# RWKV block inverse by doubling: products and copies on 64 strided columns in place of 128

## The chip, the cores and the metric

One Trainium2 chip, of which the program uses one core. The metric is the device time of one execution in microseconds; the kernel before took 3047.91 us, the median of three runs (3046.5 to 3051.92).

## The reference, cut to what matters

Two transformer blocks in float32 on 512 tokens of width 1024. The first block mixes a forgetting attention (8 heads) with an RWKV-7 recurrence (8 heads of 64) and ends with a gated feed-forward layer; the second has two further linear recurrences and a product-key mixture of 16384 experts. The change is in the RWKV recurrence alone:

```python
def step(S, inp):
    r_t, w_t, k_t, v_t, a_t, b_t = inp
    Sa = jnp.einsum('bhij,bhj->bhi', S, a_t)
    S = S * w_t[:, :, None, :] + Sa[..., None] * b_t[:, :, None, :] + v_t[..., None] * k_t[:, :, None, :]
    return S, jnp.einsum('bhij,bhj->bhi', S, r_t)
```

The kernel does not walk the 512 steps. It cuts the tokens into chunks of 64, and within a chunk the rank-one term makes a triangular system: a unit lower triangular matrix has to be inverted for each chunk and head.

## The kernel before, in words

Weights stream from HBM through a ring of tiles (`_load`, `_split`, `next_w`), and the program runs through its stages one after the other: normalisation and projections with the attention between them, then the RWKV stage, then output projection, feed-forward, the second block and the experts. Work is given in program order, but the order in which each engine gets its instructions is made when the program is built: L1679 opens the block with `schedule_with_timeline_sim=True`, and a planner orders the instructions of each engine by the times that it simulates. The splits of weights are traced at high priority. Each engine then runs its list strictly in that order and waits on semaphores.

The RWKV stage (L1576 to L1598) handles 8 units: 4 pairs of heads by 2 groups of 4 chunks. For each unit, `rwkv_elem` (once for two units) makes decays and keys, `rwkv_group` (L726 to L794) builds the matrices, among them `NT` with four blocks of 128x128, each holding two 64x64 triangles on its diagonal (the two heads), `rwkv_inv` (L796 to L832) inverts them, `rwkv_fold` multiplies the inverse into the transfer matrices (L841, L848), and `rwkv_scan` (L867) steps through the four chunks. The loop prepares unit u+2 and inverts unit u+1 while unit u is folded and scanned.

`rwkv_inv` runs for two halves of a unit side by side (`run_all`, h = 0 and 1), with two 128x128 blocks each. It keeps `T`, the inverse so far, and its transpose `Tt`. It begins with blocks of 2 (L813 to L817), and then doubles for m = 2, 4, 8, 16, 32. A level is: product `NT`ᵀ`T` for both blocks into PSUM (L809), copy to `Y` on ScalarE (L823), product `Tt`ᵀ`Y` into PSUM (L809), a masked copy into `T` on VectorE under the mask `lv` of that level (L826), and, except in the last level, two transposes (L812) and a copy to `Tt` on ScalarE (L830). The mask picks, in each square of 2m, the lower left square of m: rows of the second half, columns of the first half. All other columns of the product are computed and thrown away.

PSUM: the half h has one bank tag, `i0` in A and `i1` in B, two buffers each (L57). `cu` (L337 to L339) and `lv` (L382 to L384) are the masks, loaded from the constant `cu` in `consts` and `attn_consts` on SyncE's DMA queue; the slices of `cu` also serve `hgrn` (L1010) up to n = 32.

In the trace the digits of tile names are left out (`T0` and `T1` are `T`; the PSUM tiles `i0` and `i1` are `i`). A product in float32 stands as two weight loads and two matmul records.

Of the kernel before, what the change touches and what calls it, by code (L numbers as in the profile page):

```python
# [12 lines left out]
U32 = mybir.dt.uint32  # L13
# [46 lines left out]
def shape_consts():  # L60
    p = np.arange(128)
    out = {}
    ident = np.eye(128, dtype=np.float32)
    blk = (p[:, None] // 64 == p[None, :] // 64).astype(np.float32)
    s64 = p % 64
    t64 = np.arange(64)
    rmask = np.concatenate([s64[:, None] < t64[None], s64[:, None] <= t64[None]], 1).astype(np.float32)
    out["cf"] = np.concatenate([ident, blk, rmask, np.where(p[None] <= p[:, None], 0, -1e30).astype(np.float32)], 1)

    def lev(m, strict_same=128):  # L70
        same = p[:, None] // (2 * m) == p[None, :] // (2 * m)
        return same & (p[:, None] % (2 * m) >= m) & (p[None, :] % (2 * m) < m)
    us = [lev(m) for m in (2, 4, 8, 16, 32)] + [lev(m).T for m in (1, 2, 4, 8, 16, 32, 64)]
    out["cu"] = np.concatenate(us, 1).astype(np.uint32)
    scm = np.ones((128, T), np.float32)
    scm[:, ::64] = 0.0
    out["cs"] = scm
    out["ic"] = np.concatenate([ident[:64, :64], ident[64:, 64:]], 0)
    out["io"] = np.broadcast_to(np.arange(128, dtype=np.float32), (128, 128))
    inv = np.float32(10000.0) ** (-np.arange(128, dtype=np.float32) / np.float32(128))  # L80
    ang = np.arange(T, dtype=np.float32)[None, :] * inv[:, None]
    gam = 1.0 - 2.0 ** (-5.0 - np.arange(4))
    rel = np.arange(T)[None, :] - p[:, None]
    mr = np.where(rel[None] >= 0, gam[:, None, None] ** np.maximum(rel, 0)[None], 0.0)
    out["c2"] = np.concatenate([np.cos(ang)[None], np.sin(ang)[None], mr]).astype(np.float32)
    return out


def prep(inp):
# [58 lines left out]
    for h in range(4):  # L148
# [13 lines left out]
    o["bvec"] = np.stack([g["attn_norm_post"][0], g["ffn_norm_post"][0], g["final_norm_w_2"], g["norm_ffn_w_2"][0],  # L162
                          g["attn_norm_pre"][0], g["ffn_norm_pre"][0], g["norm_mix_w_2"][0]])
    o.update(shape_consts())
    return {k: np.ascontiguousarray(v) for k, v in o.items()}

class Prog:
# [45 lines left out]
    def v(self, name, i=0, rows=slice(0, 128)):  # L215
        o, n = VEC[name]
        return self.vec[rows, o + i:o + i + 1]
# [111 lines left out]
    def consts(self):  # L329
        nc, I, cp = self.nc, self.I, self.cp  # L330
        ld = nc.sync.dma_start
        nv = I["vec"].shape[1]
        self.vec = cp.tile([128, nv], F32, name="vec")
        ld(self.vec, I["vec"])
        self.identb = cp.tile([128, 128], BF16, name="identb")
        nc.vector.tensor_copy(self.identb, self.ident)
        self.cu = cp.tile([128, 7, 128], U32, name="cu")  # L337
        ld(self.cu, I["cu"].rearrange("p (m n) -> p m n", n=128)[:, 5:12])
        self.levTt = {1: 0, 2: 1, 4: 2, 8: 3, 16: 4, 32: 5, 64: 6}  # L339
        self.iota = cp.tile([128, 128], F32, name="iota")  # L340
        ld(self.iota, I["io"])

        dv = cp.tile([128, 56], F32, name="dv")
        self.dv = dv
        V = lambda n: self.vec[:, VEC[n][0]:VEC[n][0] + VEC[n][1]]
        ts = nc.vector.tensor_scalar
        ts(dv[:, 0:4], V("mu_r"), -1.0, 1.0, op0=ALU.mult, op1=ALU.add)
        ts(dv[:, 4:8], V("mu_k"), -1.0, 1.0, op0=ALU.mult, op1=ALU.add)
        ts(dv[:, 8:12], V("mu_v"), -1.0, 1.0, op0=ALU.mult, op1=ALU.add)
        ts(dv[:, 12:15], V("mu_l"), -1.0, 1.0, op0=ALU.mult, op1=ALU.add)  # L350
        ts(dv[:, 16:20], V("w0"), 0.5, None, op0=ALU.mult)
        ts(dv[:, 20:24], V("a0"), 0.5, None, op0=ALU.mult)
        ts(dv[:, 24:28], V("k_a"), 0.5, None, op0=ALU.mult)
        ts(dv[:, 28:29], V("fb"), -1.0, None, op0=ALU.mult)
        ts(dv[:, 32:40], V("hgw"), 0.5, None, op0=ALU.mult)

        nc.vector.tensor_tensor(dv[:, 40:48], V("lb0"), V("lb1"), op=ALU.max)
        lw = cp.tile([128, 4, 8], F32, name="lw")
        nc.vector.tensor_tensor(lw[:, 0], V("lb0"), dv[:, 40:48], op=ALU.subtract)
        nc.vector.tensor_tensor(lw[:, 1], V("lb1"), dv[:, 40:48], op=ALU.subtract)  # L360
        nc.scalar.activation(lw[:, 0:2], lw[:, 0:2], AF.Exp)
        nc.vector.tensor_tensor(lw[:, 2], lw[:, 0], lw[:, 1], op=ALU.add)
        nc.vector.reciprocal(lw[:, 2], lw[:, 2])
        nc.vector.tensor_tensor(lw[:, 3], lw[:, 0], lw[:, 2], op=ALU.mult)

        nc.vector.tensor_scalar(dv[:, 40:48], lw[:, 3], -0.5, 0.5, op0=ALU.mult, op1=ALU.add)
        nc.vector.tensor_tensor(dv[:, 48:56], lw[:, 3], dv[:, 40:48], op=ALU.add)
        self.eps = cp.tile([128, 1], F32, name="eps")
        nc.vector.memset(self.eps, NORM_EPS)
        self.ones = cp.tile([128, 128], F32R, name="ones")  # L370
        nc.scalar.activation(self.ones, self.ident, AF.Copy, bias=1.0, scale=0.0)

    def attn_consts(self):

        nc, I = self.nc, self.I
        ld = nc.sync.dma_start
        cf = self.b("ac", [128, 384])
        ld(cf, I["cf"][:, 128:512])
        self.blk, self.rmask = cf[:, 0:128], cf[:, 128:256]
        self.causb = self.b("causb", [128, 128], BF16)  # L380
        nc.vector.tensor_copy(self.causb, cf[:, 256:384])
        self.lv = self.b("lv", [128, 5, 128], U32)  # L382
        ld(self.lv, I["cu"].rearrange("p (m n) -> p m n", n=128)[:, 0:5])
        self.levT = {2: 0, 4: 1, 8: 2, 16: 3, 32: 4}  # L384
        self.ic = self.b("ic", [128, 64])
        ld(self.ic, I["ic"])
        self.cs = self.b("ac")
        ld(self.cs, I["cs"])
        self.rkblk = self.b("ac", [128, 4, 128])
        for c in range(4):  # L390
            nc.vector.tensor_scalar(self.rkblk[:, c, :], self.blk, self.v("r_k", c), None, op0=ALU.mult)
# [404 lines left out]
    def rwkv_inv(self, e, g_, h):  # L796

        nc = self.nc
        B = [128, 2, 128]
        nt = e["G", g_]["nt"][:, 2 * h:2 * h + 2]  # L800
        tt, tf = self.S(B, name=f"Tt{h}"), self.S(B, name=f"T{h}")
        mask = lambda t_, i: t_[:, i, None, :].to_broadcast(B)

        def each(op, out, *a):
            for i in range(2):
                op(out[:, i], *[x[:, i] for x in a])

        def product(out, a, b):
            nc.tensor.matmul(out, a, b, start=True, stop=True)  # L809

        def transpose(out, a):
            nc.tensor.transpose(out, a, self.ident)  # L812
        nc.gpsimd.tensor_copy(tt, self.ident[:, None, :].to_broadcast(B))  # L813
        nc.vector.copy_predicated(tt, mask(self.cu, self.levTt[1]), nt)
        pt = self.b(f"i{h}", B)
        each(transpose, pt, tt)
        nc.scalar.activation(tf, pt, AF.Copy)  # L817
        yield
        for m in (2, 4, 8, 16, 32):
            py = self.b(f"i{h}", B)  # L820
            each(product, py, nt, tf)
            y = self.S(B, name=f"Y{h}")
            nc.scalar.activation(y, py, AF.Copy)  # L823
            px = self.b(f"i{h}", B)
            each(product, px, tt, y)
            nc.vector.copy_predicated(tf, mask(self.lv, self.levT[m]), px)  # L826
            if m < 32:
                pt = self.b(f"i{h}", B)
                each(transpose, pt, tf)
                nc.scalar.activation(tt, pt, AF.Copy)  # L830
            yield
        e["G", g_]["tf", h] = tf  # L832
# [850 lines left out]
```

## Time and profile before

| what | value |
|---|---|
| median of 3 runs | 3047.91 us |
| the profiled execution, its own time | 3051.43 us |
| its span, first to last instruction | 3049.5 us |
| mean granted TensorE clock | 0.988 |
| TensorE busy with matmuls / weight loads | 2937.2 / 2539.3 us |
| VectorE, ScalarE, GpSimd busy | 1868.9, 1230.8, 1456.4 us |

PE is TensorE's matmuls, PEld its weight loads, which overlap them; DVE is VectorE, ACT ScalarE, POOL GpSimd, SP SyncE. Ends of matmuls are modelled, so the starts tell the pace better than the busy time. The page cuts the span into 40 slices of 76 us; the RWKV stage lies in the fourth to sixth, from about 240 to 450 us. PEclk is the granted clock, 1.00 for 2.4 GHz and 0.50 for 1.2 GHz.

### The profile page before, as it was taken

How to read it: one execution, taken by the hardware profiler on the slowest of the kernel's cores; microseconds unless marked ns; L12 is line 12 of the kernel's file. 1: busy time of each engine (PE TensorE's matmuls, PEld its weight loads, DVE VectorE, ACT ScalarE, POOL GpSimd, SP SyncE). 2: the span in 40 equal slices, each digit the busy share in tenths (PEclk: the TensorE clock that was granted, in tenths of full speed). 3: DMA queues.
4: the chain of work that ended last, by engine and by line, in shares of the span. 5: the costliest groups of instructions: out<-in, count | busy, mean ns of one | idle time of the engine just before them, and what ended most of it. 6: DMA issues, size and time to landing. Idle time of an engine off the chain costs nothing.

```text
span 3049.5 us, 40450 instructions
## 1 busy us (share of the span) xinstructions
PE 2937.2 (96%) x15129; PEld 2539.3 (83%) x15129; DVE 1868.9 (61%) x3173; ACT 1230.8 (40%) x1924; POOL 1456.4 (48%) x1070
## 2 busy tenths in 40 slices
PE   7998998999999999999999998998999999999998
PEld 6877787888878887888888878997899999999877
DVE  4237664444133663355532499788688777877898
ACT  5455654222232453244432334566333333333333
POOL 3223213222234562233332345676677777777764
PEclk9999999999999999999999999999999999999999
DMA  4220003333332212322233422455988888898987
GB/s 154 63 63 15 1 32 101 97 97 97 97 111 84 69 42 69 107 87 83 83 106 112 135 70 88 141 187 196 313 302 290 317 305 301 299 317 299 319 316 249
DMA packets 174355, 473.62 MB, mean 155 GB/s; under 512 B 15056, under 2 KB 64592, under 8 KB 172624
## 3 DMA queue, kind: packets, MB, share of 16 engines
q1 hardware_dynamic: 137296, 336.80, 34.0%
q0 software_dynamic: 36864, 134.23, 12.4%
q8 instruction: 120, 1.97, 0.3%
q14 instruction: 75, 0.61, 0.1%
HBM read 439.49 MB, written 31.46 MB: 154 GB/s over the span
## 4 chain that ended last, share of the span: by engine, by line
PE 63%; DVE 8%; issue 5%; DMA 4%; POOL 3%; ACT 1%; POOLq 0%; DVEq 0%; SPq 0%; ACTq 0%
PE acc L270 12%; PE acc L271 12%; PE acc L272 12%; DMA urow<-ev,ei 3%; PE A L272 3%; PE A L271 3%; PE A L270 3%; PE B L271 3%; PE B L270 3%; PE B L272 3%; PE pg L1388 2%; POOL urow L1336 1%; PE lev L986 1%; DVE mux L1315 1%; DVE wk L1233 1%
## 5 line engine op out<-in xcount | busy, mean ns | idle before, releaser
L247 POOL TENSOR_TENSOR lo<-raw,hi 128x1024 fp32r<-128x1024 f32 x224 | 557.1, 2488 | 819.0 <-ACT hi L244 783.2
L270 PE MATMUL acc<-u,hi 128*128 128x512 f32 (+3 forms) x2344 | 859.4, 367 | 12.5 <-ACT x L1403 8.6
L271 PE MATMUL acc<-u,hi 128*128 128x512 f32 (+3 forms) x2344 | 856.6, 366 | 0.2 <-DVE u L476 0.2
L272 PE MATMUL acc<-u,lo 128*128 128x512 f32 (+3 forms) x2344 | 855.5, 365 | 0.0
L244 ACT ACTIVATE hi<-raw 128x1024 fp32r<-128x1024 f32 x447 | 473.2, 1059 | 882.9 <-PE acc L271 446.7
L270 PEld LDWEIGHTS acc<-u,hi 128*128 128x128 f32 (+1 forms) x2344 | 444.5, 190 | 67.4 <-ACT x L1403 9.2
L247 DVE TENSOR_TENSOR lo<-raw,hi 128x1024 fp32r<-128x1024 f32 x223 | 311.6, 1398 | 297.4 <-ACT hi L244 297.1
L271 PEld LDWEIGHTS acc<-u,hi 128*128 128x128 f32 (+1 forms) x2344 | 444.6, 190 | 53.8 <-issue 2.7
L272 PEld LDWEIGHTS acc<-u,lo 128*128 128x128 f32 (+1 forms) x2344 | 444.2, 190 | 49.1 <-issue 0.6
L1344 DVE SCALAR_TENSOR_TENSOR urow<-urow,h4row 128x1024 f32<-128x1024 f32 x128 | 201.0, 1578 | 90.9 <-DMA urow<-eu,ei 90.2
L1354 DVE SCALAR_TENSOR_TENSOR po<-urow,act,po 128x1024 f32<-128x1024 f32 x127 | 200.8, 1581 | 71.7 <-DMA urow<-ev,ei 70.6
L1336 POOL DMA_INDIRECT urow<-eu,ei x128 | 188.5, 1472 | 33.1 <-issue 23.7
L1414 ACT ACTIVATE wh<-wf 128x384 fp32r<-128x384 f32 x128 | 67.4, 528 | 322.0 <-PE D L271 244.6
L1336 POOL DMA_INDIRECT urow<-ev,ei x128 | 174.4, 1362 | 44.8 <-DVE po L1354 18.7
L247 POOL TENSOR_TENSOR lox<-rawx,hix 128x1024 fp32r<-128x1024 f32 x53 | 138.4, 2612 | 96.5 <-ACT hix L244 96.2
L1390 ACT ACTIVATE gstage<-pg 128x512 f32<-128x512 f32 x96 | 99.1, 1107 | 60.3 <-PE pg L1388 59.7
L1379 DVE TENSOR_SCALAR ohA<-iota,slT 128x128 f32<-128x128 f32 x384 | 117.4, 371 | 2.3 <-ACT slT L1364 1.1
L1388 PE MATMUL pg<-ohB,ohA 128*128 128x128 f32 x768 | 100.4, 278 | 15.1 <-DVE ohB L1385 7.7
L1388 PEld LDWEIGHTS pg<-ohB,ohA 128*128 128x128 f32 x768 | 94.8, 191 | 19.7 <-ACT gstage L1390 10.5
L1383 POOL TENSOR_SCALAR ohB<-iota,slT 128x128 f32<-128x128 f32 x144 | 95.9, 681 | 26.4 <-PE pg L1388 26.4
L1415 DVE TENSOR_TENSOR wl<-wf,wh 128x384 fp32r<-128x384 f32 x128 | 98.9, 774 | 5.7 <-ACT wh L1414 3.8
L1385 DVE TENSOR_TENSOR ohB<-iota,slT 128x512 f32<-128x512 f32 x60 | 66.4, 1107 | 33.7 <-PE pg L1388 33.5
(573 smaller groups left out, 5473.5 us busy)
## 6 DMA issues: line engine op xcount, KB each, us to landing
raw<-ut SPq DMA_DIRECT2D x128, 512.0 KB
raw<-ev SPq DMA_DIRECT2D x75, 512.0 KB
rawx<-ev SPq DMA_DIRECT2D x53, 512.0 KB
raw<-w_ret SPq DMA_DIRECT2D x48, 512.0 KB
gd<-gstage SPq DMA_DIRECT2D x12, 2048.0 KB
gread<-gd SPq DMA_DIRECT2D x32, 768.0 KB
raw<-w_gu SPq DMA_DIRECT2D x44, 512.0 KB
raw<-w_hg SPq DMA_DIRECT2D x32, 512.0 KB
```

The costliest lines, as they stand in the source:

```text
L244: self.nc.scalar.activation(hi, raw, AF.Copy)
L247: r = eng.tensor_tensor(lo, raw, hi.bitcast(F32), op=ALU.subtract)
L270: mm(out, a[0], b[0], start=start, stop=False)
L271: mm(out, a[0], b[1], start=False, stop=False)
L272: return mm(out, a[1], b[0], start=False, stop=stop).ins
L1336: r = nc.gpsimd.indirect_dma_start(out=u, out_offset=None, in_=src, in_offset=bass.IndirectOffsetOnAxis(ap=ei[:, s:s + 1], axis=0))
L1344: nc.vector.scalar_tensor_tensor(u, u, 1.0, row, op0=ALU.mult, op1=ALU.mult, accum_out=act[:, s:s + 1])
L1354: nc.vector.scalar_tensor_tensor(o, u, act[:, s:s + 1], o, op0=ALU.mult, op1=ALU.add)
L1379: nc.vector.tensor_scalar(A4[:, r], self.iota, sl[:, 0, k + r:k + r + 1], sl[:, 2, k + r:k + r + 1], op0=ALU.is_equal, op1=ALU.mult)
L1388: last = nc.tensor.matmul(p[:, r, :], A4[:, r], B4[:, r], start=True, stop=True)
L1390: nc.scalar.activation(st[:, :, q * 4:q * 4 + 4].rearrange("p j t -> p t j"), p, AF.Copy)
L1415: nc.vector.tensor_tensor(wl, wf, wh.bitcast(F32), op=ALU.subtract)
```

## The change

In each level only the columns that the mask can pick are computed: the first m columns of every 2m, 64 of 128. `T` is viewed as blocks of 2m columns and `first` is the first half of each. The first product takes `first` as its moving operand, with gaps; its output, `Y`, the second product and its output are dense tiles of 64 columns for each of the two blocks. The masked copy goes from the dense product into `first`, with gaps, under masks of 64 columns, which are a new constant `cl`. The stationary operands (`NT`, `Tt`) stay 128x128, and transposes and the copies to `Tt` stay as they are. The constant `cu` keeps six slices (it had twelve, of which seven and five were loaded).

```diff
--- before.py
+++ after.py
@@ -70,8 +70,11 @@
     def lev(m, strict_same=128):
         same = p[:, None] // (2 * m) == p[None, :] // (2 * m)
         return same & (p[:, None] % (2 * m) >= m) & (p[None, :] % (2 * m) < m)
-    us = [lev(m) for m in (2, 4, 8, 16, 32)] + [lev(m).T for m in (1, 2, 4, 8, 16, 32, 64)]
+    us = [lev(m).T for m in (1, 2, 4, 8, 16, 32)]
     out["cu"] = np.concatenate(us, 1).astype(np.uint32)
+
+    out["cl"] = np.concatenate([lev(m).reshape(128, 64 // m, 2, m)[:, :, 0].reshape(128, 64) for m in (2, 4, 8, 16, 32)],
+                               1).astype(np.uint32)
     scm = np.ones((128, T), np.float32)
     scm[:, ::64] = 0.0
     out["cs"] = scm
@@ -334,9 +337,9 @@
         ld(self.vec, I["vec"])
         self.identb = cp.tile([128, 128], BF16, name="identb")
         nc.vector.tensor_copy(self.identb, self.ident)
-        self.cu = cp.tile([128, 7, 128], U32, name="cu")
-        ld(self.cu, I["cu"].rearrange("p (m n) -> p m n", n=128)[:, 5:12])
-        self.levTt = {1: 0, 2: 1, 4: 2, 8: 3, 16: 4, 32: 5, 64: 6}
+        self.cu = cp.tile([128, 6, 128], U32, name="cu")
+        ld(self.cu, I["cu"].rearrange("p (m n) -> p m n", n=128))
+        self.levTt = {1: 0, 2: 1, 4: 2, 8: 3, 16: 4, 32: 5}
         self.iota = cp.tile([128, 128], F32, name="iota")
         ld(self.iota, I["io"])
 
@@ -379,8 +382,8 @@
         self.blk, self.rmask = cf[:, 0:128], cf[:, 128:256]
         self.causb = self.b("causb", [128, 128], BF16)
         nc.vector.tensor_copy(self.causb, cf[:, 256:384])
-        self.lv = self.b("lv", [128, 5, 128], U32)
-        ld(self.lv, I["cu"].rearrange("p (m n) -> p m n", n=128)[:, 0:5])
+        self.lv = self.b("lv", [128, 5, 64], U32)
+        ld(self.lv, I["cl"].rearrange("p (m n) -> p m n", n=64))
         self.levT = {2: 0, 4: 1, 8: 2, 16: 3, 32: 4}
         self.ic = self.b("ic", [128, 64])
         ld(self.ic, I["ic"])
@@ -799,34 +802,35 @@
         B = [128, 2, 128]
         nt = e["G", g_]["nt"][:, 2 * h:2 * h + 2]
         tt, tf = self.S(B, name=f"Tt{h}"), self.S(B, name=f"T{h}")
-        mask = lambda t_, i: t_[:, i, None, :].to_broadcast(B)
-
-        def each(op, out, *a):
+        C = [128, 2, 64]
+
+        def product(out, a, b):
             for i in range(2):
-                op(out[:, i], *[x[:, i] for x in a])
-
-        def product(out, a, b):
-            nc.tensor.matmul(out, a, b, start=True, stop=True)
+                nc.tensor.matmul(out[:, i], a[:, i], b[:, i], start=True, stop=True)
 
         def transpose(out, a):
-            nc.tensor.transpose(out, a, self.ident)
+            for i in range(2):
+                nc.tensor.transpose(out[:, i], a[:, i], self.ident)
         nc.gpsimd.tensor_copy(tt, self.ident[:, None, :].to_broadcast(B))
-        nc.vector.copy_predicated(tt, mask(self.cu, self.levTt[1]), nt)
+        nc.vector.copy_predicated(tt, self.cu[:, self.levTt[1], None, :].to_broadcast(B), nt)
         pt = self.b(f"i{h}", B)
-        each(transpose, pt, tt)
+        transpose(pt, tt)
         nc.scalar.activation(tf, pt, AF.Copy)
         yield
         for m in (2, 4, 8, 16, 32):
-            py = self.b(f"i{h}", B)
-            each(product, py, nt, tf)
-            y = self.S(B, name=f"Y{h}")
+
+            first = tf.rearrange("p i (b two m) -> p i b two m", two=2, m=m)[:, :, :, 0, :]
+            v = lambda a: a.rearrange("p i (b m) -> p i b m", m=m)
+            py = self.b(f"i{h}", C)
+            product(v(py), nt, first)
+            y = self.S(C, name=f"Y{h}")
             nc.scalar.activation(y, py, AF.Copy)
-            px = self.b(f"i{h}", B)
-            each(product, px, tt, y)
-            nc.vector.copy_predicated(tf, mask(self.lv, self.levT[m]), px)
+            px = self.b(f"i{h}", C)
+            product(px, tt, y)
+            nc.vector.copy_predicated(first, v(self.lv[:, self.levT[m], None, :].to_broadcast(C)), v(px))
             if m < 32:
                 pt = self.b(f"i{h}", B)
-                each(transpose, pt, tf)
+                transpose(pt, tf)
                 nc.scalar.activation(tt, pt, AF.Copy)
             yield
         e["G", g_]["tf", h] = tf
```

## Rows read from the trace of the kernel before

**Rows 1.** The page, parts 1 and 2: TensorE's busy share and granted clock in 40 slices.
```profile
PE 2937.2 (96%) x15129; PEld 2539.3 (83%) x15129; DVE 1868.9 (61%) x3173; ACT 1230.8 (40%) x1924; POOL 1456.4 (48%) x1070
PEclk9999999999999999999999999999999999999999
```

**Rows 2.** The chain of waits, its first piece: start us, us, what.
```profile
507.22 0.75 DVE xs L467
```

**Rows 3.** Stretches, 240 to 450 us: length, busy us (instructions) of each engine, PEclk, DMA.
```profile
240.00:450.00 210.00, 194.69 (x1386) 164.05 (x1385) 145.66 (x323) 132.06 (x338) 47.25 (x72) 0.96 0.03 9
```

**Rows 4.** Groups by line, 240 to 450 us: busy us, mean ns, idle before and releasers.
```profile
L809 PE MATMUL i<-Y,Tt 128*128 128x128 f32 x320 | 51.3, 288 | 1.1 <-ACT Y L823 1.0
L809 PE MATMUL i<-T,NT 128*128 128x128 f32 x320 | 50.6, 282 | 0.0
...
L823 ACT ACTIVATE Y<-i 128x256 f32<-128x256 f32 x80 | 30.7, 384 | 6.6 <-PE i L809 5.6
```

**Rows 5.** Order of time, 304 to 309 us: start us, us, engine, line, work, count.
```profile
304.82 0.56 PE L867 MATMUL ys<-SV,M 128*128 128x64 f32 x4
...
306.78 0.61 PE L809 MATMUL i<-T,NT 128*128 128x128 f32 x4
...
307.34 0.53 PEld L809 LDWEIGHTS i<-T,NT 128*128 128x128 f32 x4
307.78 0.53 PEld L867 LDWEIGHTS ys<-SV,M 128*128 128x128 f32 x4
308.23 0.86 PEld L809 LDWEIGHTS i<-Y,Tt 128*128 128x128 f32 x7
```

**Rows 6.** Single lines and the tile lv: ns min/median/max, first and last start us, form.
```profile
L826 DVE COPY_PREDICATED T<-lv,i x80: 422/444/455, 257.3 to 438.6; 128x256 f32<-128x256 uint32 x80
L383 SPq DMA_DIRECT2D lv<-cu x1: 327/327/327, 12.2 to 12.2; - x1
...
L793 ACT ACTIVATE SV<-gv x32: 270/272/276, 237.0 to 411.9; 64x128 f32<-64x128 f32 x32
...
L1300 DVE COPY_PREDICATED ab<-cm,cu x4: 284/295/300, 1784.1 to 1898.2; 128x128 uint32<-128x128 uint32 x4
...
L1029 DVE TENSOR_TENSOR qp<-qp,tot x56: 399/426/2625, 950.6 to 1155.5; 128x256 f32<-128x256 f32 x56
```

**Rows 7.** Waits of TensorE, 243 to 445 us: us in total, times, longest us.
```profile
PEld i L812 <- DVE T L826: 6.1, 11, 0.9
...
PEld i L809 <- ACT Y L823: 4.2, 10, 0.8
...
PEld ga L783 <- ACT M L766: 1.9, 4, 1.0
...
PEld i L812 <- DVE ld L674: 1.5, 1, 1.5
...
PE i L812 <- DVE T L826: 2.9, 6, 0.7
...
PE i L809 <- ACT Y L823: 1.0, 3, 0.5
```

**Rows 8.** Stretches around the falls of the clock, columns as in rows 3.
```profile
237.00:250.00 13.00, 10.77 (x33) 6.80 (x34) 12.51 (x21) 7.42 (x20) 7.51 (x13) 0.50 0.14 42
...
322.00:326.00 4.00, 1.99 (x12) 1.48 (x13) 1.99 (x4) 3.58 (x7) 0.00 (x0) 0.95 0.00 0
326.00:329.00 3.00, 3.00 (x13) 2.48 (x12) 2.77 (x6) 0.39 (x1) 0.00 (x0) 0.50 0.00 0
329.00:380.00 51.00, 48.24 (x359) 40.74 (x358) 35.71 (x81) 33.17 (x88) 13.63 (x21) 1.00 0.00 1
...
384.00:387.00 3.00, 3.00 (x13) 2.36 (x11) 2.88 (x7) 0.56 (x2) 0.00 (x0) 0.50 0.00 0
```

**Rows 9.** Stretches in which VectorE is nearly always busy, columns as in rows 3.
```profile
257.00:275.00 18.00, 14.30 (x106) 11.81 (x105) 17.67 (x37) 10.72 (x29) 3.53 (x5) 1.00 0.00 1
...
329.00:340.00 11.00, 10.32 (x84) 8.99 (x82) 10.71 (x23) 7.18 (x20) 1.47 (x2) 1.00 0.00 0
```

## The prediction, made before the changed kernel was run

> **What bounds the kernel now.** I read the page first: TensorE is busy 96% of the span and its clock is granted almost throughout [rows 1], so the kernel is a string of stages that TensorE paces, and a change is worth what it does to TensorE's stream in its own stage. The chain of waits begins only at 507 us and from there is nearly all matmuls [rows 2]; it is no witness for the stage of this change, so that stage has to be read from its own rows. The view of stretches gives it: from 240 to 450 us, where the RWKV blocks are built, inverted and scanned, TensorE shows 194.7 of 210 us busy and VectorE 145.7 [rows 3]. At most 15.3 us of TensorE's time is open there, and nothing behind the stage can gain: what ends sooner here moves the rest forward as it is.
>
> The inverse makes 80 half-levels (8 units, 2 halves, 5 levels). Each has four products, which stand in the groups of lines as 8 matmul records, one ScalarE copy Y and one masked VectorE copy [rows 4]; the two halves of a unit run side by side, so there are 40 levels in a row.
>
> **The products.** Every product streams 64 columns in place of 128; its stationary side keeps 128 x 128. The kernel already has such a group: the scan's `ys`, 128 x 128 stationary with 64 columns. In the order of time, its four weight loads start 0.45 us ahead of the next group's (307.78 to 308.23), and the four of a 128-column product 0.44 us ahead (307.34 to 307.78) [rows 5]. The stream is paced by weight loads, 0.11 us a record, and half the columns leave that pace as it is. What shortens is the end of a group: 0.61 us from its first start to its last end with 128 columns, 0.56 with 64 [rows 5]. I take 0.05 us per group of four, and only where somebody waits for the group.
>
> In the Trainium skill, "TensorE: Matmul & The Clock Gate", section "Back-to-back issue gap", the gap of an isolated matmul is its columns over the clock plus a small constant, by which half the columns would take about half; the same page's section "LDWEIGHTS (loading the stationary operand)" lets the load go by the stationary columns, which do not change. By the first the sum would be that of rival C; the scan's row sides with the second.
>
> **The copies.** Y shrinks from 128x256 to 128x128: 0.384 us now [rows 4], 0.272 for a ScalarE copy of 128 columns out of PSUM [rows 6], so 0.11 less. The masked copy shrinks likewise: 0.444 now, 0.295 for one of 128x128, so 0.15 less [rows 6]. The target is now strided (runs of m in blocks of 2m). The nearest row is L1029, which reads and writes such half blocks of 256 elements: 0.426, no more than a dense copy of that size [rows 6]; I take nothing for the stride. For the strided moving operand of TensorE there is no row. Bounds: nothing, or all that the halving brings, since 64 columns with gaps span the 128 read now. I take nothing, being nearest to the VectorE row. In sum ScalarE loses 80 x 0.11 = 9 us of work and VectorE 80 x 0.15 = 12 us; neither bounds the stage as a whole. VectorE does so locally, 17.67 of 18 us at 257 to 275 and 10.71 of 11 at 329 to 340 [rows 9].
>
> **The constants.** The two mask loads stay two loads in their places on the SP queue, with fewer bytes. `lv` is issued at 12.2 us and first read at 257.3 [rows 6]; I cost this at nothing, and 245 us of other work cover it. Transposes, their copies Tt, and the first level are untouched.
>
> **The sum.** One level's chain becomes shorter by 2 x 0.05 + 0.11 + 0.15 = 0.36 us. Were all 40 levels waited for throughout, that is 14.4 us, close to the 15.3 us that TensorE has open: the end of what can be gained. The waits say how often a level is waited for: TensorE's loads waited for the masked copy 11 times (6.1 us) and for Y 10 times (4.2 us); the matmuls themselves name them 6 times (2.9) and 3 times (1.0), which overlap the former [rows 7]. Each wait averages 0.4 to 0.55 us, longer than its cut, so the cut counts whole: 11 x (0.05 + 0.15) + 10 x (0.05 + 0.11) = 3.8 us, and 5.5 if the other nine stand apart. I take 3.8, because the two lists largely show the same stalls. What is late next is work of other units, `M` from ScalarE (1.9 us in 4 waits) and `ld` from VectorE (1.5 us in one) [rows 7]. The gain's lower end is zero, if the shorter step only uncovers these. The profiled execution took 3051.43 us (span 3049.5 and 1.9 around it); 3051.4 - 3.8 = 3047.6. That execution lies 3.5 us above the median of 3047.91, so against the median it is 3044.1.
>
> The build orders each engine's instructions by its own simulated times (L1679), so shorter operations may give another order in this stage. It can close open time or open more; the 14.4 us above bound the good side.
>
> **Rivals.** 0.2% is 6.1 us here, about what a measurement can tell from no change: faster means below 3041.8, slower above 3054.0.
>
> *A. The order closes most of the open time.* With 12 us less on VectorE, and it the bound at 257 to 275 and 329 to 340 [rows 9], the levels draw together and more waits go than the counted 21. Against it: TensorE's weight loads alone keep it full elsewhere. About 10 of the 14.4 us: 3038.
>
> *B. TensorE's clock.* It stood at 1.2 GHz from 237 to 250 us, at 326 to 329 and at 384 to 387, and the fall at 326 came behind a stretch in which the engine was busy 1.99 of 4 us [rows 8]. Half-width passes leave the array idle for part of every load, so in a loosely filled stretch it may be taken for idle, and once at 1.2 GHz half-width passes do less to lift it again. Price: 326 to 329 held 13 records in 3 us, 329 to 380 held 359 in 51, 21 per 3 us [rows 8]; a microsecond at 1.2 GHz costs 0.4 to 0.5 us. Up to 8 us more of it only eat the gain: 3048. From some 20 us more it decides: 10 us lost against 3.8 gained, over 3054; with 25 us 3047.9 - 3.8 + 12.5 = 3056.6. For it: TensorE is 14.3 of 18 busy at 257 to 275 [rows 9]. Against it: from 329 to 380 the engine is 48.2 of 51 us busy and the clock stays at 2.4 GHz [rows 8], and most of the stage is like that and not like what stood ahead of the fall.
>
> The same page of the Trainium skill, section "The HAM clock gate (the \"warmup\" mystery)", says the slow clock is the default and activity releases it; whether half-streamed passes count in full no run here shows.
>
> *C. A product goes by its columns after all.* 640 records at 0.11 us, halved: 35 us, 3013. The scan's row speaks against it.
>
> *D. The change doesn't save.* A moving operand read with gaps takes as long as the full one, or the chain is hidden wherever it shortens: 3048.
>
> **How the numbers follow.** Forecast as summed, gain of 0 to 6 us: 0.42. A, 0.29. B slower, 0.15; B eating the gain, 0.08. C, 0.03. D, 0.03. Faster is A and C, 0.32; same is the forecast, mild B and D, 0.53; slower is 0.15. The likeliest case gives 3044, its own range 3042 to 3048. The range for 8 in 10 reaches through most of A (3035, 13 us gained) and up to B with some 24 us of low clock (3056); C and the ends of A and B are left out.
>
> **What would show it.** Right: L809's records stay 320 and 320 with loads 0.11 us apart and groups end at 0.56; Y near 0.27 and the masked copy near 0.30, alike for m = 2 and 32; TensorE's waits on Y and the masked copy fall from 10.3 us to about 6; the stage ends some 4 us earlier and all behind it is as long as before. Wrong: loads 0.06 us apart (C); clock below 1.00 in stretches now at 1.00 (B); a masked copy or product that is dearer at m = 2 (D); another order of units in the stage (A or worse), or a later stage of another length.

## The result, and the profile of the changed kernel

The changed kernel takes 3078.49 us (median of 8 runs, 3052.43 to 3092.08); the kernel before, run beside it, 3049.91 (8 runs, 3045.88 to 3053.82). The ratio is 1.0086, interval 1.0068 to 1.0103: 28.6 us slower by the medians. The forecast was 3044, its range ended at 3056: it was wrong, and on the side of rival B. The profiled execution took 3075.0 us, with a span of 3073.2 and a mean granted clock of 0.976.

First the page, TensorE's share and clock, to be set beside [rows 1]:

```profile
PE 2964.1 (96%) x15129; PEld 2570.8 (84%) x15129; DVE 1861.8 (61%) x3173; ACT 1221.4 (40%) x1924; POOL 1448.8 (47%) x1070
PEclk9995889999999999999999999999999999999999
```

The engine is as full as before, but three slices of the clock have fallen, and they are the slices of the RWKV stage. The counts of instructions are the same. VectorE and ScalarE have 7 and 9 us less to do, so the shorter copies are there.

The kernel behind 240 us in two stretches, cut at the first `sil` of the feed-forward layer (517 us before, 547 after); columns as in [rows 3]. The kernel before:

```profile
240.00:517.00 277.00, 253.81 (x1694) 213.59 (x1692) 177.53 (x376) 162.14 (x400) 71.73 (x90) 0.96 0.11 33
517.00:3049.00 2532.00, 2463.74 (x12321) 2150.34 (x12321) 1597.72 (x2647) 954.61 (x1303) 1313.21 (x891) 0.99 0.52 175
```

The changed kernel:

```profile
240.00:547.00 307.00, 284.49 (x1695) 248.54 (x1693) 171.36 (x377) 154.50 (x400) 71.96 (x90) 0.82 0.10 30
547.00:3073.00 2526.00, 2459.94 (x12321) 2147.05 (x12321) 1597.11 (x2647) 953.03 (x1303) 1305.80 (x891) 0.99 0.53 175
```

The same products (1694 and 1695 matmul records) take 277 us before and 307 after, and the clock of that stretch falls from 0.96 to 0.82. What lies behind is 6 us shorter, no more than the 8 us by which the runs of the kernel before differ among themselves. So the loss is in the first of the two, which holds the RWKV stage.

Inside the stage, the stretch of [rows 3] and then its pieces, each at one level of the clock:

```profile
240.00:450.00 210.00, 196.06 (x1171) 172.12 (x1170) 123.56 (x283) 106.36 (x292) 43.84 (x68) 0.76 0.01 3
...
237.00:261.00 24.00, 21.78 (x82) 16.29 (x82) 18.73 (x34) 12.29 (x32) 10.59 (x19) 0.51 0.08 23
261.00:267.00 6.00, 4.04 (x16) 1.89 (x16) 2.18 (x6) 4.83 (x8) 1.13 (x1) 1.00 0.00 0
268.00:318.00 50.00, 49.23 (x237) 47.57 (x236) 22.58 (x56) 17.80 (x55) 4.74 (x9) 0.50 0.00 1
...
350.00:363.00 13.00, 13.00 (x65) 12.32 (x64) 9.84 (x24) 5.47 (x16) 0.00 (x0) 0.50 0.00 0
364.00:407.00 43.00, 40.65 (x312) 35.17 (x311) 24.91 (x61) 26.54 (x75) 13.30 (x21) 1.00 0.01 2
408.00:424.00 16.00, 15.69 (x70) 14.01 (x71) 11.73 (x28) 6.07 (x19) 0.92 (x2) 0.50 0.00 0
425.00:467.00 42.00, 40.38 (x341) 38.16 (x340) 22.50 (x61) 21.91 (x70) 5.88 (x8) 1.00 0.01 2
```

The kernel before stood at 1.2 GHz for 13 + 3 + 3 = 19 us [rows 8]; this one for 24 + 50 + 13 + 16 = 103, which is 84 us more. The row from 268 to 318 matters most. TensorE was busy 49.23 of 50 us, waited for another engine once (0.8 us, for `M` from ScalarE), and stayed at 1.2 GHz all the same, ahead of it only a loose piece (4.04 of 6 us). In that piece of 50 us it made 237 records, from 364 to 407 us at 2.4 GHz 312 in 43 us: 4.7 a microsecond against 7.3, so a microsecond at 1.2 GHz loses 0.35 of one. The stage itself, from the first load of its products to its last masked copy, went from 190.2 us (248.4 to 438.6) to 217.8 (249.3 to 467.1). That is 27.6 us for 84 us of low clock, 0.33 each.

The single operations. Tile `i` and its readers: duration in ns (min/median/max), first and last start, form.

```profile
L809 PE MATMUL i<-T,NT x320: 222/275/473, 249.6 to 465.3; 128*128 128x64 f32 x160
...
L827 ACT ACTIVATE Y<-i x80: 258/277/312, 252.0 to 466.0; 128x128 f32<-128x128 f32 x80
L830 DVE COPY_PREDICATED T<-lv,i x80: 277/296/483, 257.0 to 467.1; 128x128 f32<-128x128 uint32 x80
```

The median of the masked copy hides one level. At m = 2, where the target has runs of two columns, all 16 copies take 0.42 to 0.48 us, as long as the copies of 256 elements before (0.444 [rows 6]); at the other four levels they take 0.28 to 0.30. In the order of time, two of m = 2 and then two of m = 4:

```profile
375.52 0.44 DVE L830 COPY_PREDICATED T<-lv,i 128x128 f32<-128x128 uint32 x1 [1.05 <-PE i L809]
...
376.42 0.44 DVE L830 COPY_PREDICATED T<-lv,i 128x128 f32<-128x128 uint32 x1 [0.15 <-PE i L809]
...
378.55 0.29 DVE L830 COPY_PREDICATED T<-lv,i 128x128 f32<-128x128 uint32 x1 [0.77 <-PE i L809]
...
380.51 0.29 DVE L830 COPY_PREDICATED T<-lv,i 128x128 f32<-128x128 uint32 x1
```

And loads and products in the order of time, first a piece at 1.2 GHz, then one at 2.4:

```profile
302.49 0.98 PEld L809 LDWEIGHTS i<-T,NT 128*128 128x128 f32 x4
303.35 0.97 PEld L809 LDWEIGHTS i<-Y,Tt 128*128 128x128 f32 x4
...
364.98 0.53 PEld L809 LDWEIGHTS i<-T,NT 128*128 128x128 f32 x4
365.42 0.53 PEld L809 LDWEIGHTS i<-Y,Tt 128*128 128x128 f32 x4
...
365.09 0.56 PE L809 MATMUL i<-T,NT 128*128 128x64 f32 x4
```

At 2.4 GHz four loads take 0.44 us (364.98 to 365.42), which is the pace of 128 columns in [rows 5], and a group of four ends after 0.56. At 1.2 GHz four loads take 0.86.

One more thing has to be known before the experiments. The 8 runs are of one program, in one order of instructions, and yet they spread over 40 us. Their mean clocks go with it: the two lowest times, 3052.43 and 3059.11, have a clock of 0.983; the other six, 3075.0 to 3092.08, have 0.972 to 0.977.

### The profile page after: what moved, and what is told of

It is laid out like the page before. It is cut to its first block, busy times and chain, and to the rows that moved or that the text cites. A ratio compares the mean times of both kernels' runs of the same rounds, so it can differ in the third digit from the quotient of the medians.

```text
span 3073.2 us, 40438 instructions
## 1 busy us (share of the span) xinstructions
PE 2964.1 (96%) x15129; PEld 2570.8 (84%) x15129; DVE 1861.8 (61%) x3173; ACT 1221.4 (40%) x1924; POOL 1448.8 (47%) x1070
## 4 chain that ended last, share of the span: by engine, by line
PE 84%; DVE 9%; issue 3%; ACT 2%; DMA 1%; POOL 1%; SPq 0%; DVEq 0%; POOLq 0%; ACTq 0%
PE acc L273 15%; PE acc L274 15%; PE acc L275 15%; PE A L275 3%; PE A L274 3%; PE A L273 3%; PE B L274 3%; PE B L273 3%; PE B L275 3%; PE i L809 2%; PE pg L1392 2%; PE lev L990 1%; DVE mux L1319 1%; PE C L275 1%; PE C L273 1%
## 5 line engine op out<-in xcount | busy, mean ns | idle before, releaser
L250 DVE TENSOR_TENSOR lo<-raw,hi 128x1024 fp32r<-128x1024 f32 x223 | 318.2, 1427 | 302.4 <-ACT hi L247 302.1
L1358 DVE SCALAR_TENSOR_TENSOR po<-urow,act,po 128x1024 f32<-128x1024 f32 x127 | 193.3, 1522 | 64.5 <-DMA urow<-ev,ei 63.8
```

Source lines behind the costliest of these rows:

```text
L250: r = eng.tensor_tensor(lo, raw, hi.bitcast(F32), op=ALU.subtract)
L1358: nc.vector.scalar_tensor_tensor(o, u, act[:, s:s + 1], o, op0=ALU.mult, op1=ALU.add)
```

## The experiments

Three explanations were open. The **clock**: the narrow products themselves bring the low clock. The **gaps**: a moving operand read with gaps is what costs. The **order**: shorter operations gave the planner another order, and that one is worse. All seven kernels compute the whole result; `filler` adds products that nobody reads. The diffs are against the changed kernel. Four kernels (`full_dense`, `full_gaps`, `second_full`, `products_alone`) shared one set of runs of the kernel before (3048.23, median of 29), the other three (`first_full`, `filler`, `narrow_Tt`) another (3047.5, median of 21).

**All columns back, the short copies kept** (`full_dense`). Both products stream 128 columns again, the second the same 64 twice; Y and the masked copy take only the 64 that count.

```diff
-            py = self.b(f"i{h}", C)
-            product(v(py), nt, first)
+            py = self.b(f"i{h}", B)
+            product(py, nt, tf)
...
-            nc.scalar.activation(y, py, AF.Copy)
-            px = self.b(f"i{h}", C)
-            product(px, tt, y)
+            nc.scalar.activation(v(y), py.rearrange("p i (b two m) -> p i b two m", two=2, m=m)[:, :, :, 0, :], AF.Copy)
+            px = self.b(f"i{h}", B).rearrange("p i (two n) -> p i two n", two=2)
+            product(px, tt, y[:, :, None, :].to_broadcast([128, 2, 2, 64]))
```

The masked copy reads `px[:, :, 0, :]`.

> The changed kernel with its short copies (Y and masked copy of 64 columns), but each product streams 128 columns again: the first over all of T, with ScalarE picking the 64 wanted columns out of PSUM; the second streams the 64 columns of Y twice. The useful work and the copies are those of the changed kernel. Clock theory (64-column products let TensorE's clock fall): the granted clock from 240 to 450 us is back near 0.96 (0.76 in the changed kernel) and the time is at or below that of before, 3041 to 3050. Order theory (shorter operations led the build to a worse order of instructions in the stage): the shorter copies still change the order, and the time stays some 15 to 30 us above before, 3065 to 3080. Gap theory (a moving operand read with gaps is dear): as the clock theory in time, since the gaps are gone here, but then the variant that streams all 128 columns with gaps stays slow.

Measured: 3045.64 us (12 runs, 3042.97 to 3051.76), ratio to before 1.0000, interval 0.9991 to 1.0008. Its stretch and its operations:

```profile
240.00:450.00 210.00, 193.08 (x1392) 164.86 (x1393) 137.75 (x322) 121.90 (x335) 46.52 (x70) 0.97 0.03 9
...
L827 ACT ACTIVATE Y<-i x80: 257/278/298, 250.8 to 434.8; 128x128 f32<-128x128 f32 x80
L830 DVE COPY_PREDICATED T<-lv,i x80: 273/297/490, 254.7 to 436.0; 128x128 f32<-128x128 uint32 x80
```

The copies are as short as in the changed kernel, the clock of the stretch is back at 0.97 and the loss is gone. What costs is the narrowing of the products, not the copies and not the constants.

**All columns back, with gaps** (`full_gaps`). As above, but the first product reads `T` in the order of the changed kernel, first halves and then second halves.

```diff
+            product(py.rearrange("p i (two b m) -> p i two b m", two=2, m=m), nt,
+                    tf.rearrange("p i (b two m) -> p i two b m", two=2, m=m))
+            nc.scalar.activation(y, py[:, :, 0:64], AF.Copy)
```

> As the variant with 128 streamed columns, but the first product streams T with gaps: first the first halves of all blocks, then the second halves, so that Y is a dense read of PSUM. Clock theory: like its sibling within 3 us, clock from 240 to 450 us near 0.96. Gap theory: the first product's records are longer than 275 ns at m = 2 and the time lies 10 us or more above its sibling. Order theory: 3065 to 3080.

Measured: 3048.42 us (11 runs, 3044.62 to 3052.64), ratio 1.0004, interval 0.9995 to 1.0012. Every engine has its instructions in the same order as in the experiment before, by operation and tile name, so the two differ only in which read has the gaps (TensorE's of `T` here, ScalarE's of PSUM there), and a product has the same length:

```profile
L809 PE MATMUL i<-T,NT x320: 273/275/422, 248.9 to 437.4; 128*128 128x128 f32 x160
```

The line mixes the levels; by the shapes in the trace, the first product's records at m = 2 and at 2.4 GHz have the same median of 275 ns. Gaps in the moving operand cost nothing that can be measured in these products, which their weight loads pace: the explanation falls.

**One product of the two.** `second_full` takes the second product's lines of `full_dense`, `first_full` the first product's lines of `full_gaps`; the other product stays at 64 columns.

> The changed kernel with only the second product streaming 128 columns (Y twice); the first still streams 64 with gaps. Clock theory: between the two, clock from 240 to 450 us between 0.80 and 0.96, time 3045 to 3070, since half of what was taken away is back. Gap theory: as slow as the changed kernel, 3075 to 3080, for the gaps stay. Order theory: no forecast of its own, 3065 to 3080.

> The mirror of the kernel with the second product full: only the first product streams 128 columns (all of T, first halves first), the second streams the 64 columns of Y. Clock theory: what counts is how much is streamed, not which product: like its mirror, 3045 to 3056, clock from 240 to 450 us 0.90 to 0.96. Theory that the first product's gapped read or its place in the chain is what hurts: all of the loss is gone, 3042 to 3049; and the mirror should have been slow, which it wasn't.

Measured: 3051.41 us (10 runs, 3049.79 to 3054.3), ratio 1.0010, interval 1.0000 to 1.0020; and 3051.63 us (10 runs, 3049.75 to 3058.25), ratio 1.0017, interval 1.0008 to 1.0026. The stretch of the first:

```profile
240.00:450.00 210.00, 193.25 (x1383) 166.38 (x1382) 136.74 (x320) 120.11 (x334) 47.99 (x72) 0.94 0.03 7
```

and of the second:

```profile
240.00:450.00 210.00, 192.38 (x1362) 163.97 (x1362) 134.03 (x316) 120.11 (x333) 46.34 (x70) 0.92 0.03 7
```

It makes no difference that can be measured which product is narrow. One narrow product costs 3 to 4 us by the medians (0 to 6 and 2 to 8 by the intervals), far less than half of 28.6. The loss does not grow evenly with the number of narrow products.

**The products narrow, the copies long** (`products_alone`). The other half of the change by itself: both products at 64 columns, but Y written twice (256 elements) and the masked copy over all columns under full masks.

```diff
-            y = self.S(C, name=f"Y{h}")
-            nc.scalar.activation(y, py, AF.Copy)
+            y = self.S([128, 2, 2, 64], name=f"Y{h}")
+            nc.scalar.activation(y, py[:, :, None, :].to_broadcast([128, 2, 2, 64]), AF.Copy)
...
-            product(px, tt, y)
-            nc.vector.copy_predicated(first, v(self.lv[:, self.levT[m], None, :].to_broadcast(C)), v(px))
+            product(px, tt, y[:, :, 0, :])
+            w = lambda x: x.rearrange("p i (b two m) -> p i b two m", two=2, m=m)
+            nc.vector.copy_predicated(w(tf), w(self.lv[:, self.levT[m], None, :].to_broadcast(B)),
+                                      v(px)[:, :, :, None, :].to_broadcast([128, 2, 64 // m, 2, m]))
```

> The other half of the change alone: products of 64 columns as in the changed kernel, but Y and the masked copy at their full 256 elements a partition again (Y written twice side by side, the product read twice under the old 128-column masks). Clock theory: the clock falls as in the changed kernel or more, since the longer copies leave TensorE idle longer; clock from 240 to 450 us at or below 0.80, time 3075 to 3095. Order theory: the copies cost the planner what they did before, so much of the old order comes back and the time is nearer to before, 3050 to 3065. Gap theory: 3075 to 3085.

Measured: 3089.46 us (4 runs, 3058.97 to 3102.8), ratio 1.0106, interval 1.0069 to 1.0144. The run of 3058.97 has a clock of 0.982, the others, 3086.66 to 3102.8, of 0.965 to 0.971. The stretch, and the longest piece at 1.2 GHz:

```profile
240.00:450.00 210.00, 197.16 (x958) 169.39 (x956) 112.08 (x241) 100.20 (x250) 36.58 (x59) 0.62 0.01 3
...
266.00:357.00 91.00, 90.23 (x405) 82.89 (x405) 39.14 (x89) 36.02 (x95) 11.76 (x21) 0.50 0.00 1
```

The loss comes with the products alone. With the copies long again, TensorE stood at 1.2 GHz for 91 us at a stretch, busy 90.23 of them, in the profiled execution (the one of 3102.8 us).

**More work for TensorE** (`filler`). The changed kernel with one product more in each half-level: 128 columns, written into a part of PSUM that nobody reads.

```diff
-            px = self.b(f"i{h}", C)
+            pb = self.b(f"i{h}", B).rearrange("p i (two n) -> p i two n", two=2)
+            nc.tensor.matmul(pb[:, :, 1, :], nt[:, 0], tf[:, 0].rearrange("p (two n) -> p two n", two=2), start=True, stop=True)
+            px = pb[:, :, 0, :]
```

> The changed kernel, its 64-column products untouched, with work added: per level and half one more float32 product of 128 columns (two loads, 0.22 us of TensorE's stream, 160 records and some 18 us in all) that reads T and writes PSUM which nobody reads; it can run while TensorE would wait for Y. Clock theory: the added stream holds the clock up, 0.88 or more from 240 to 450 us, and the kernel with more work is faster than the changed one, 3048 to 3068. Theory that the slower time comes from the order or from the narrow products as such: the added work comes on top, 3085 to 3100.

Measured: 3066.05 us (5 runs, 3065.2 to 3067.97), ratio 1.0059, interval 1.0045 to 1.0072, all five runs at a clock of 0.984 or 0.985. Its stretch, and the added group (L829):

```profile
240.00:450.00 210.00, 199.46 (x1442) 173.25 (x1441) 129.69 (x302) 114.47 (x318) 45.45 (x70) 0.91 0.01 4
...
L829 PE MATMUL i<-T,NT x160: 272/275/527, 250.5 to 454.1; 128*128 128x128 f32 x160
```

The filler's 160 records at 0.11 us are 17.6 us of work, and the kernel is 18.5 us above before: the work is paid for and nearly nothing else. Added to a loss that stayed as it was, it would have given 28.6 + 17.6 = 46 us. The low clock has mostly gone, and so has the spread of the runs. That the kernel with the useless work is faster than the changed one (18.5 against 28.6 us) is likely but not shown: the intervals of the two ratios just meet.

**A shorter copy to Tt** (`narrow_Tt`). `full_dense`, and the copy to `Tt` takes only the columns of the second halves, the only ones that change in a level.

```diff
-                nc.scalar.activation(tt, pt, AF.Copy)
+                w = lambda x: x.rearrange("p i (b two m) -> p i b two m", two=2, m=m)[:, :, :, 1, :]
+                nc.scalar.activation(w(tt), w(pt), AF.Copy)
```

> The variant with 128 streamed columns and short copies, and in addition the copy of the transpose takes only the second halves of the blocks (64 of 128 columns, the only ones that a level changes): 64 ScalarE copies go from 0.38 to about 0.28 us in the chain of levels, nothing changes on TensorE. If copies in the chain are worth their cut where TensorE waits: 2 to 4 us under its sibling, 3041 to 3045. If TensorE's waits only pass on to other work, as with the first two copies: within 2 us of it, 3044 to 3048. If loosening the chain lets the clock fall: 3050 or more.

Measured: 3046.77 us (11 runs, 3042.67 to 3050.59), ratio 0.9992, interval 0.9983 to 1.0001. The copy:

```profile
L835 ACT ACTIVATE Tt<-i x64: 258/278/292, 259.3 to 435.3; 128x128 f32<-128x128 f32 x64
```

By its ratio it is the best version tried, by the medians `full_dense` is; neither is clear of the kernel before.

All together. The time at 1.2 GHz is worked out from the clock of the stretch 240 to 450 us, as 210 x 2 x (1 - clock). It leaves out what lies behind 450 us, and the clock is that of the one profiled execution. The excess is the median over that of before in the same set.

| kernel | columns, first and second product | at 1.2 GHz, us | stage, us | excess, us |
|---|---|---|---|---|
| before | 128, 128 | 17 | 190.2 | 0 |
| narrow_Tt | 128, 128 | 17 | 187.1 | -0.7 |
| full_dense | 128, 128 | 13 | 187.9 | -2.6 |
| full_gaps | 128, 128 | 25 | 190.5 | 0.2 |
| second_full | 64, 128 | 25 | 189.2 | 3.2 |
| first_full | 128, 64 | 34 | 192.6 | 4.1 |
| filler | 64, 64, and 128 more | 38 | 205.6 | 18.5, of them 17.6 its own work |
| changed | 64, 64 | 101 | 217.8 | 28.6 |
| products_alone | 64, 64 | 160 | 243.5 | 41.2 |

**The order.** The planner works with other times for each kernel, so all but the two full ones differ from each other in the order of this stage. Four things speak against it as the cause. The changed kernel's 8 runs, in one order, lie 40 us apart and follow the clock. The kernels of the table, in several orders, come roughly in the sequence of their time at 1.2 GHz. An order unlike the one of before is not dear by itself: counted by operation and tile name, TensorE's matmuls of the changed kernel differ from those of before in 830 of 15129 places, those of `full_dense` in 866, and `full_dense` has no loss. And the changed kernel and `first_full` share their order for nearly the whole stage: by the same names (which leave out the digits) their first 2258 matmul records stand in one sequence, up to 447.1 us in the changed kernel and 421.2 in `first_full`, and up to there only one pair of neighbours each has changed places on VectorE, on ScalarE and among the weight loads. The piece between the same two matmul records in both, first the changed kernel, then `first_full`:

```profile
252.20:447.10 194.90, 183.18 (x1115) 163.09 (x1115) 112.27 (x262) 96.61 (x267) 37.38 (x56) 0.77 0.00 1
...
251.70:421.20 169.50, 154.44 (x1115) 132.01 (x1115) 111.31 (x262) 96.23 (x265) 37.75 (x56) 0.94 0.00 1
```

The same 1115 matmul records in the same order take 25.4 us less when the first product streams 128 columns, and that is all of the difference between these two profiled executions (3075.0 and 3050.09). The loss goes with the number of streamed columns and the clock, not with the order. That the order decides where the clock first falls stays possible, and why the low clock lasts is open.

## Why the prediction was wrong, point by point

**The products: right.** The stream is paced by weight loads, 0.44 us for four, whether 64 or 128 columns follow, and a group's end is 0.05 us earlier (0.56 against 0.61, minima of 222 against 273 to 275 ns). So rival C is out, and its 35 us did not come. The Trainium skill, "TensorE: Matmul & The Clock Gate", section "LDWEIGHTS (loading the stationary operand)", lets the load go by the stationary columns; by that the pace could not change, and the trace agrees.

**The copies: right in size but for one level.** Y takes 0.277 us (0.272 forecast). The masked copy takes 0.296 (0.295) at four of the five levels; at m = 2 it takes 0.44 and saves nothing, where the prediction took nothing for the stride. Its row L1029 has copies of several block sizes in one median and could not show this. So VectorE's masked copies fell from 34.8 us of busy time to 25.6, by 9 and not by 12; the time of the kernel doesn't hang on it, since the same copies stand in `full_dense`. Gaps in the moving operand, taken at nothing, cost nothing that the runs can tell. **The constants**, taken at nothing too, are part of every experiment, and the full ones show no loss.

**The gain of 3.8 us: not shown.** `full_dense` has the short copies and a clock of 0.97 in the stretch, and its ratio leaves 2.7 us of gain to 2.4 of loss. Its waits, columns as in [rows 7]:

```profile
PEld i L813 <- DVE T L830: 4.0, 6, 0.9
PEld i L809 <- ACT Y L827: 3.6, 9, 0.8
```

The two waits fell from 10.3 to 7.6 us, where 6 were forecast. In the changed kernel itself they are shorter than forecast, 3.9 us, but there TensorE was the slower one for 103 us:

```profile
PEld i L809 <- ACT Y L827: 2.4, 5, 0.8
...
PEld i L813 <- DVE T L830: 1.5, 4, 0.5
```

The stage of `full_dense` is 2.3 us shorter than before, that of `full_gaps`, with the same copies and the same order, 0.3 us longer. If the gain is there, it is at most of the forecast size and below what the runs can tell.

**The step that failed is the sum: it set the clock's term at zero.** It added up what each level's chain saves and let everything run at the clock of before; a lower clock stood only in rival B, at 0.15. In the changed kernel that term is 84 us more at 1.2 GHz, and the stage became 27.6 us longer (at the 0.35 us of the two rates above it would be 29), seven times the gain.

**Rival B had the mechanism and lost by its counter-argument.** It said that most of the stage is like 329 to 380 us, 48.2 of 51 us busy [rows 8], and that a stretch so full stays at 2.4 GHz. That row was of 128-column products, and the argument moved it unchanged to 64. After the change a stretch of 50 us, busy 49.23, stood at 1.2 GHz; B, too, had looked for the low clock in loosely filled stretches only. The busy time could not witness for the clock: a matmul record stands with a median of 275 ns at 64 columns as at 128, at 2.4 GHz alone too, so that half the columns do not show in it. B's other numbers: it needed 20 us more of low clock to decide and got 84; its price of 0.4 to 0.5 us (its own rows, 13 records against 21, give 0.38) was too high against the 0.33 measured. The stage at 2.4 GHz is not all weight loads, 35.17 of 43 us from 364 to 407 against 47.57 of 50 from 268 to 318, which would explain it. With that price, and 3.8 us gained, it would have taken (6.1 + 3.8) / 0.33 = 30 us.

The Trainium skill, "TensorE: Matmul & The Clock Gate", section "The HAM clock gate (the "warmup" mystery)", says that the slow clock is the default and that activity releases it. The experiments agree so far as restored columns, or added products, brought the clock back. What is meant by activity no run here shows: from 268 to 318 us the profile has TensorE busy 49.23 of 50 us, and the clock stayed at 1.2 GHz.

**A** did not come: even with the clock back, the stage of `full_dense` is 2.3 us shorter and not 10. **D** had a masked copy that is dearer at m = 2, and that came; its dear moving operand did not, and the change did not come out even.

## What to carry to other kernels

When a product's pace is set by its weight load, cutting the columns that it streams saves next to nothing and can cost the clock; look at the granted clock of the stage, and not at TensorE's busy share, before and after such a cut. Keep the full width in the product and cut the copies that read it: that cost nothing here, though no gain was clear of noise either. Look at a strided copy at its shortest runs, and not at the median over all levels. If the runs of one program spread by over 1%, set their mean clocks beside their times before anything is explained by the instructions.

## What the runs showed of the hardware that was not expected

- TensorE can be busy almost without a gap and stay at 1.2 GHz: 49.23 of 50 us in the changed kernel, 90.23 of 91 in `products_alone`. In the same kernel the same products also ran at 2.4 GHz for 42 us (425 to 467), so narrow products do not always bring the fall. What ends a low stretch was not found.
- How long the low clock lasts differs from run to run of one program: 3052 to 3092 us for the changed kernel, 3059 to 3103 for `products_alone`, with the mean clock going along. With 160 more full-width records the spread was 2.8 us.
- One narrow product of the two costs 3 to 4 us, both cost 28.6.
- A masked VectorE copy of 128 elements a partition out of PSUM takes 0.44 us when the target has runs of two columns, as long as one of 256 without gaps; with runs of 4 to 32 it takes 0.28 to 0.30 us.
